# Two norms in front of a SwiGLU: more output blocks in halves, gate products tile by tile, squares summed on TensorE

## The chip, the cores and the metric

The kernel runs on one core of a Trainium2 chip. The metric is the device time of one execution in microseconds (us); a lower time is better. The engines are PE (matrix products; PEld is its weight load), DVE, ACT and POOL (elementwise work), and SP, which here only issues transfers. Every engine works through its own instructions in order; semaphores make one wait for another.

## The reference

One layer of a hybrid encoder over 576 columns (512 of a prompt, 64 of a running stream), model width 1024, feed-forward width 2816:

```python
h = rms_norm(x, g_pre_mix)
p = h @ w_in                       # RWKV-7 rows | gMLP u, v | two gates
o_a = rwkv7(...)                   # recurrence over chunks
o_b = gmlp(...)                    # spatial gating
m = sigmoid(pga) * (o_a @ w_proj_a) + sigmoid(pgb) * (o_b @ w_proj_b)
x = x + rms_norm(m @ w_o, g_post_mix)
f = rms_norm(x, g_pre_ffn)
f = (silu(f @ w_gate) * (f @ w_up)) @ w_down
x = x + rms_norm(f, g_post_ffn)
```

The change lies between `m @ w_o` and the first blocks of `f @ w_gate` and `f @ w_up`.

## The kernel before

All data is transposed: rows of 128 features on the partitions, T = 576 columns beside each other, in two halves of HALF = 288. A product in fp32 precision is made of three cheaper ones: both factors are split into a high part (`h`, `whi`) and the rest (`l`, `wlo`), and high x high, low x high and high x low are added up in PSUM. So a block of 128 output features by one half of the columns takes 8 tiles of 128 input features x 3 = 24 matmuls of 288 columns, and a whole block 48.

**Weights.** `todo` lists the weight blocks in the order of use. `ahead` loads the next one (`raw`) by SP; `split_next()` splits the oldest one that is loaded: ACT writes the high part (L302) and POOL the rest in two pieces of 512 columns (L305), into a ring of three buffers for each (`whi`, `wlo`), or into buffers of its own (`own`, called `s` in the profile). `EARLY` names w_o blocks that are split during the `pb` products (`o_b @ w_proj_b`), and `STEPS` says at which w_o product how many further blocks are split.

**Order.** `behind` writes the second part of the layer down: `pa` and `pb` products, w_o products (`po`), the first gate and up products (`fp`, NF = 2 of 22 blocks), the main loop of them (`fg`), w_down. It is a generator. A planner (`Weave`) runs it beside other generators (`norm1`, `norm2`, `hidden` and more), each of which yields the time or the event at which it is due (`LAT` holds assumed latencies). So the order on PE is the planner's, fixed when the kernel is built. ACT, DVE and POOL take the order that the tile scheduler gives them, except where `keep_in_program_order` pins it.

**w_o and norm1.** `normed_product` computes the first 8 - NLAST blocks whole; then the last NLAST = 5 blocks for the first half of the columns, and then for the second half. `evac1` brings each result from PSUM to `y[j]` (ACT, L1308) and its squares to `zb` (ACT, L1289), which DVE adds up in `gin` (L1290, `acc1`). When a half is done, `norm1(h)` sums the squares over the partitions (three matmuls with one column on a vector of ones, `rs`), takes the power on POOL (`rr`, L368), broadcasts it with three matmuls (`rb`), and then makes, tile by tile, y*rb (DVE, L1321), + x (DVE, L1324), the high part f0h to f7h (ACT, L1325) and the low part f0l to f7l (DVE, L1328). `fcount` counts the tiles that are there.

**First gate products.** For each half, each of the two blocks and gate and up, `half_product("fp", ...)` takes the eight f tiles in order, with one PSUM bank at a time. The four banks of a half come one after the other.

**norm2.** The scale of the second norm (`rs2`) is not applied to f but later, in `swiglu`. For `norm2(h)`, for each y tile, ACT squares it into `zb` and POOL adds it to a second `gin` (`acc2`, L1290 again); then three `rs` matmuls, the power and the broadcast as in norm1. The `hidden` generator starts `swiglu` for the two first blocks once their products and `rs2` are there, and writes their results `d0`, `d1`.

Of the kernel before, what the change touches and what calls it, by code (L numbers as in the profile page):

```python
# [5 lines left out]
F32 = mybir.dt.float32  # L6
F32R = mybir.dt.float32r
ACT = mybir.ActivationFunctionType
ALU = mybir.AluOpType
# [3 lines left out]
P = 128  # L13
D = 1024
TS = 64
TP = 512
T = TS + TP
HALF = T // 2
# [7 lines left out]
KD = D // P  # L26
RMS_EPS = 1e-6
# [206 lines left out]
def layer(tc, I, O):  # L234
# [3 lines left out]
    pe, dve, act, pool, sp = nc.tensor, nc.vector, nc.scalar, nc.gpsimd, nc.sync  # L238
# [7 lines left out]
    nb = {"a": 4}  # L246
# [15 lines left out]
    def ps1(name, hold=0.0):  # L262
        clk.take(hold)
        return psum.tile([P, 512], F32, tag="a", bufs=nb["a"], name=name)
# [7 lines left out]
    def mmul(out, lhsT, rhs, **kw):  # L272
        n = 1
        for d in rhs.shape[1:]:
            n *= d
        rows = lhsT.shape[0]
        if rows != clk.rows:
            clk.now += 0.12
            clk.rows = rows
        if rhs.dtype == F32R:  # L280
            clk.now += 0.011 + n / 2400
        elif rows == P:
            clk.now += max(n, P) / 600
        else:
            clk.now += n / 2000 if rows == 64 else 0.037 if rows == 32 else 0.02
        return pe.matmul(out, lhsT, rhs, **kw)  # L286
# [69 lines left out]
    def rstd_cols(out, m, sq, starts, s=None, more=None):  # L356

        s = ps1("rs") if s is None else s  # L360
        n = len(starts)
        for j, t0 in enumerate(starts):
            mmul(s[:, j:j + 1], sq[:, t0:t0 + P], one, start=True, stop=more is None)
            if more is not None:
                mmul(s[:, j:j + 1], more[:, t0:t0 + P], one, start=False, stop=True)
            clk.now += 0.1
        dve.tensor_scalar(m[:, 0:n], s[:, 0:n], 1.0 / D, RMS_EPS, ALU.mult, ALU.add)
        pool.tensor_tensor(out[:, 0:n], m[:, 0:n], mhalf[:, 0:n], ALU.pow)  # L368
# [19 lines left out]
    def until(*ev):  # L388
        while ev not in clk.events:
            yield True  # L390
# [669 lines left out]
    def slot(i, dt=F32):  # L1060

        return R["gp"].tile([P, D], dt, tag=f"s{i}", bufs=1, name=f"s{i}")
# [49 lines left out]
    def mixed(name, **kw):  # L1112
        return R["mp"].tile([P, T], F32, tag=name, name=name, **{"bufs": 1, **kw})
# [105 lines left out]
            yield LAT["zz"]  # L1219


    NLAST, NF = 5, 2
    EARLY = {3: 6, 5: 7}
    STEPS = {(0, 0): 1, (1, 0): 1, (2, 0): 2, (3, 0): 1, (4, 1): 1, (5, 1): 1, (6, 1): 1, (7, 1): 1}

    def own(i):
        return lambda: (slot(2 * i, F32R), slot(2 * i + 1, F32R))

    todo = [(("w_proj_a", j), I["w_proj_a"][j], None) for j in range(8)]
    for j in range(8):  # L1230
        todo.append((("w_proj_b", j), I["w_proj_b"][j], None))
        if j - 1 in EARLY:
            i = EARLY[j - 1]
            todo.append((("w_o", i), I["w_o"][i], own(i - 6)))
    todo += [(("w_o", j), I["w_o"][j], None) for j in range(6)]
    todo += [((n, j), I[n][j], own(0) if (j, n) == (NF - 1, "w_up") else None) for j in range(NFF) for n in ("w_gate", "w_up")]
    last_w = lambda k0: lambda: [R["op"].tile([P, min(KD, NFF - k0) * P], F32R, name=f"w{k0}{n}") for n in "hl"]
    todo += [(("w_down", j), I["w_down"][j][:, k0 * P:min(k0 + KD, NFF) * P], last_w(k0) if j == 6 else None) for j in range(8) for k0 in range(0, NFF, KD)]
# [15 lines left out]
    def half_product(name, wb, xs, kts, h, step=None, ready=lambda k: True, cut=HALF):  # L1254
        dst = psum.tile([P, 512], F32, tag="h", bufs=6, name=name)[:, 0:(cut, T - cut)[h]]
        for k in range(kts):
            while not ready(k):
                yield True
            if step is not None and k % KD == 0:
                step()  # L1260
            mm({h: dst}, wb, xs[0], xs[1], k, kts, halves=(h,), cut=cut)
            yield
        return dst
# [19 lines left out]
    def square_sum(q, acc, src, first, hs, eng=dve):  # L1283

        if first:
            act.activation(acc[:, hs], src, ACT.Square)
        else:
            q = q()
            act.activation(q[:, hs], src, ACT.Square)  # L1289
            eng.tensor_tensor(acc[:, hs], acc[:, hs], q[:, hs], ALU.add)  # L1290

    def rstd_row(p, acc, starts, tag, more=None):

        m = p.tile([P, 3], F32, tag=tag + "m", bufs=2, name="rm")
        r = p.tile([P, 3], F32, tag=tag + "r", bufs=2, name="rr")
        rstd_cols(r, m, acc, starts, more=more)
        yield LAT["rb"]
        b = ps1("rb")
        for j, t0 in enumerate(starts):
            t0 -= starts[0]  # L1300
            mmul(b[:, t0:t0 + P], r[:, j:j + 1].broadcast_to([P, P]), ident, start=True, stop=True)
        return b[:, 0:starts[-1] + P - starts[0]]

    mix_q = lambda: mixed("zb", bufs=2)
    y, xt = [], []

    def evac1(j, ps, hs):
        act.activation(y[j][:, hs], ps, ACT.Copy, scale=V("g_post_mix", j))  # L1308
        square_sum(mix_q, R["acc1"], ps, j == 0, hs)

    fcount = [0, 0]

    def norm1(h):
        hs = HS[h]
        yield (("po", h), LAT["rs"])
        b = yield from rstd_row(R["fp"], R["acc1"], STARTS[h], "r1")
        keep = tc.keep_in_program_order
        fh, fl = fs
        for j in range(10):
            if j < 8:  # L1320
                keep(dve.tensor_tensor(y[j][:, hs], y[j][:, hs], b, ALU.mult))  # L1321
            if 1 <= j < 9:
                i = j - 1
                keep(dve.tensor_tensor(y[i][:, hs], y[i][:, hs], xt[i][:, hs], ALU.add))  # L1324
                act.activation(fh[i][:, hs], y[i][:, hs], ACT.Copy, scale=V("g_pre_ffn", i))  # L1325
            if j > 1:
                i = j - 2
                keep(dve.scalar_tensor_tensor(fl[i][:, hs], y[i][:, hs], V("g_pre_ffn", i), f(fh[i][:, hs]), ALU.mult, ALU.subtract))  # L1328
                fcount[h] = i + 1
            yield LAT["f0"] if j == 0 else LAT["f"]  # L1330
        clk.signal("y", h)

    def norm2(h):
        hs = HS[h]
        yield (("y", h), 0.0)
        for j in range(8):
            square_sum(mix_q, R["acc2"], y[j][:, hs], j == 0, hs, pool)
            yield LAT["sq"]
        yield LAT["rs"]
        b = yield from rstd_row(R["fp"], R["acc2"], STARTS[h], "r2")  # L1340
        act.activation(R["rs2"][:, hs], b, ACT.Copy)
        clk.signal("rs2", h)


# [50 lines left out]
    def norm3(h):  # L1395
        hs = (slice(0, CUT), slice(CUT, T))[h]
        yield (("pd", h), LAT["rs"])
        y2, x1 = R["yw"][:, :, hs], R["xw"][:, :, hs]
        b = yield from rstd_row(R["op"], R["acc3"], ENDS[h], "r3", R["sq7"])
        keep = tc.keep_in_program_order  # L1400
        for j0, j1, eng in ((0, 2, pool), (2, 4, pool), (4, 6, dve), (6, 8, dve)):
            js = slice(j0, j1)
            keep(dve.tensor_tensor(y2[:, js], y2[:, js], b.unsqueeze(1).broadcast_to([P, j1 - j0, hs.stop - hs.start]), ALU.mult))
            keep(eng.tensor_tensor(y2[:, js], y2[:, js], x1[:, js], ALU.add))
            sp.dma_start(O["yT"][js, :, hs].rearrange("j p t -> p j t"), y2[:, js])


    def behind(ws, split_next):
# [1 line left out]
        clk.signal("behind")  # L1410
        ps_es.close()
        ps_es, psum = mk("ps2", space=PSUM)
        nb["a"] = 2
        ps1("rs")

        def pa_done(j, t, ps):
            o = half_sum(j)
# [28 lines left out]
            dve.tensor_tensor(ma[j], ma[j], t, ALU.add)  # L1446
            keepers(ms, split(R["mp"], ma[j], f"m{j}", scale=0.5))
        y[:] = [half_sum(j) for j in range(8)]
        R["acc1"], R["acc2"] = [mixed("gin", bufs=2) for _ in range(2)]
        R["rs2"] = R["fp"].tile([P, T], F32, name="rs2")  # L1450
        for j in range(8):
            if j < 3:
                xt.append(slot(4 + j))
            elif j < 5:
                xt.append(R["mp"].tile([P, D], F32, tag=("bias", "wsT")[j - 3], bufs=1, name="xt"))
            elif j < 7:
                xt.append(mixed("xt", bufs=2))
            else:
                xt.append(R["fp"].tile([P, T], F32, name="xt"))
            sp.dma_start(xt[j][:, 0:T], I["xT"][:, j, :])  # L1460
# [4 lines left out]
        for j in range(NF):  # L1465
            for x, n in zip(ds, "hl"):
                x.append(R["dp0"].tile([P, T], F32R, name=f"d{j}{n}"))
        for h in range(2):
            for j in range(NF):
                halfway[h, j] = []  # L1470
                for n in ("w_gate", "w_up"):
                    if (h, j, n) == (1, 1, "w_gate"):
                        yield from until("d", 0, 0)
                    if h == 1:
                        yield from until("y", 0)
                    ps = yield from half_product("fp", ws[n, j], fs, KD, h, None, lambda k: fcount[h] > k)
                    halfway[h, j].append(ps)
                    if h == 1:
                        split_next()
                clk.signal("fp", h, j)  # L1480
        for j in range(NF, NFF):
            pgu = []
# [56 lines left out]
```

## Time and profile before

| | us |
|---|---|
| median of 3 runs | 1239.83 (1239.71 to 1240.45) |
| profiled execution | 1237.7 |
| its span | 1235.9 |
| mean granted clock of PE | 0.984 |
| first gate product to first of the main loop | 786.90 to 824.76 |

A row of the timeline gives start, length, engine, line and operation with the tiles that it writes and reads (`fp<-f4l,whi`: into fp from f4l and the weights whi), and in brackets how long the engine was idle before it and what ended that. All matmuls have the line L286, that of a helper. Lengths of matmuls overlap; starts tell their pace. PEclk is the clock granted to PE, 1.00 being full.

### The profile page before, as it was taken

The numbers are of one execution on the slowest core, as the hardware profiler recorded it, in microseconds if no ns is written. First come the engines' busy times: TensorE is split into PE (matmuls) and PEld (weight loads), VectorE is DVE, ScalarE is ACT, GpSimd is POOL, SyncE is SP. The second block draws the span as 40 slices with busy tenths as digits, with TensorE's granted clock in tenths as the row PEclk, the third lists the DMA queues.
The fourth block names the chain that finished last, engine by engine and source line by source line (L and its number), as shares of the span: only waits on it lengthen the run. The fifth ranks groups of instructions, "written<-read, shape, count | busy, mean of one in ns | idle before, by whom it ended". The sixth has DMA issues, their size and how long they took to land.

```text
span 1235.9 us, 29949 instructions
## 1 busy us (share of the span) xinstructions
PE 1187.6 (96%) x12926; PEld 1154.5 (93%) x12926; DVE 547.8 (44%) x1081; ACT 466.1 (38%) x889; POOL 614.1 (50%) x484
## 2 busy tenths in 40 slices
PE   7989999989999989899899999899999999999997
PEld 6989898889899989899899999899999999999996
DVE  5756556665555565632624431654333333300003
ACT  5555544443545434333431233442222222222220
POOL 6665354635354545333445553566565555634442
PEclk9999999998999999999999999899999999999998
DMA  5233222222222222231554542232222222252222
GB/s 184 81 106 90 72 82 85 73 70 67 72 82 85 82 63 72 79 97 63 174 173 129 181 141 86 69 128 85 74 82 86 86 86 85 69 168 83 78 77 77
DMA packets 68276, 118.05 MB, mean 96 GB/s; under 512 B 30832, under 2 KB 36208, under 8 KB 68144
## 3 DMA queue, kind: packets, MB, share of 16 engines
q1 hardware_dynamic: 68000, 116.06, 30.9%
q8 instruction: 101, 1.65, 0.6%
q14 instruction: 31, 0.25, 0.1%
q10 hardware_dynamic: 144, 0.08, 0.0%
HBM read 99.83 MB, written 16.28 MB: 94 GB/s over the span
## 4 chain that ended last, share of the span: by engine, by line
PE 76%; DVE 13%; ACT 3%; issue 3%; POOL 3%; DMA 2%; SPq 0%; DVEq 0%; POOLq 0%; ACTq 0%
PE fg L286 20%; PE pj L286 16%; PE po L286 15%; PE pb L286 4%; PE gv L286 4%; PE pa L286 3%; POOL wlo L305 2%; DVE X L865 2%; DVE Xt L862 2%; PE am L286 2%; PE z L286 1%; PE d L286 1%; DVE TD L965 1%; PE pc L286 1%; DVE y L1324 1%
## 5 line engine op out<-in xcount | busy, mean ns | idle before, releaser
L305 POOL TENSOR_TENSOR wlo<-raw,whi 128x512 fp32r<-128x512 f32 (+1 forms) x288 | 400.5, 1413 | 374.2 <-ACT whi L302 344.3
L302 ACT ACTIVATE whi<-raw 128x1024 fp32r<-128x1024 f32 x144 | 149.7, 1046 | 279.6 <-PE fg L286 174.6
L1290 DVE TENSOR_TENSOR rs<-rs,nsq 128x288 f32<-128x288 f32 (+2 forms) x12 | 9.0, 754 | 105.9 <-ACT nsq L1289 105.9
L1358 DVE TENSOR_TENSOR ft<-ft,fg 128x288 f32<-128x288 f32 x40 | 16.4, 451 | 68.0 <-PE fg L286 66.5
L1352 DVE TENSOR_TENSOR fg<-fg,rs 128x288 f32<-128x288 f32 x40 | 16.5, 453 | 63.2 <-PE fg L286 63.1
L1355 DVE SCALAR_TENSOR_TENSOR ft<-ft,fg 128x576 f32<-128x576 f32 (+1 forms) x24 | 28.7, 1197 | 19.0 <-ACT ft L1354 19.0
L1356 POOL TENSOR_TENSOR ft<-ft,rs 128x576 f32<-128x576 f32 (+1 forms) x24 | 31.8, 1327 | 7.1 <-DVE ft L1355 7.1
L286 PE MATMUL pc<-S,TD 128*128 128x64 f32 x112 | 20.9, 270 | 13.1 <-DVE So L1004 10.8
L286 PEld LDWEIGHTS pc<-S,TD 128*128 128x128 f32 x112 | 18.3, 198 | 15.6 <-DVE So L1004 12.2
L865 DVE TENSOR_TENSOR X<-X,Xt 80x15 f32<-80x15 f32 (+7 forms) x120 | 29.4, 245 | 3.9
L862 DVE TENSOR_TENSOR Xt<-X,M 80x15 f32<-80x15 f32 (+7 forms) x120 | 29.3, 245 | 3.6
L1035 POOL TENSOR_TENSOR gm<-gm,mhalf 128x10 f32<-128x10 f32 x8 | 16.2, 2022 | 27.3 <-DVE gm L1034 27.2
L1004 DVE TENSOR_TENSOR S<-pc,C 128x64 f32<-128x64 f32 x48 | 10.5, 219 | 42.8 <-PE pc L286 42.8
L286 PE MATMUL pj<-h5h,whi 128*128 128x288 f32 x88 | 28.4, 323 | 0.0
L765 POOL TENSOR_TENSOR BK<-BK,EL 128x576 f32<-128x576 f32 x16 | 19.8, 1238 | 16.9 <-PE am L286 16.9
L286 PE MATMUL pj<-h0h,whi 128*128 128x288 f32 x88 | 28.2, 320 | 0.0
L286 PE MATMUL pj<-h6h,whi 128*128 128x288 f32 x88 | 28.1, 320 | 0.0
L286 PE MATMUL pj<-h3h,whi 128*128 128x288 f32 x88 | 27.9, 317 | 0.0
L286 PE MATMUL pj<-h7h,whi 128*128 128x288 f32 x88 | 27.7, 315 | 0.0
L286 PE MATMUL pj<-h1h,whi 128*128 128x288 f32 x88 | 27.6, 314 | 0.0
L286 PE MATMUL pj<-h2h,whi 128*128 128x288 f32 x88 | 27.6, 314 | 0.0
L286 PE MATMUL pj<-h4h,whi 128*128 128x288 f32 x88 | 27.6, 313 | 0.0
(1200 smaller groups left out, 4281.4 us busy)
## 6 DMA issues: line engine op xcount, KB each, us to landing
raw<-in_w_in SPq DMA_DIRECT2D x50, 512.0 KB, 3.7
raw<-in_w_gate SPq DMA_DIRECT2D x22, 512.0 KB, 3.7
raw<-in_w_up SPq DMA_DIRECT2D x22, 512.0 KB, 3.6
raw<-in_w_down SPq DMA_DIRECT2D x16, 512.0 KB, 3.5
raw<-in_w_gv SPq DMA_DIRECT2D x8, 512.0 KB, 3.6
raw<-in_w_proj_a SPq DMA_DIRECT2D x8, 512.0 KB, 3.8
raw<-in_w_proj_b SPq DMA_DIRECT2D x8, 512.0 KB, 3.7
raw<-in_w_o SPq DMA_DIRECT2D x8, 512.0 KB, 3.7
```

Source lines behind the costliest of these rows:

```text
L286: return pe.matmul(out, lhsT, rhs, **kw)
L302: keep(act.activation(hi[:, :cols], raw[:, :cols], ACT.Copy))
L305: keep(pool.tensor_tensor(lo[:, c0:c1], raw[:, c0:c1], f(hi[:, c0:c1]), ALU.subtract))
L765: pool.tensor_tensor(by_chunk(BK[:, x, :]), by_chunk(BK[:, x, :]), EL[:, :, 64:65].broadcast_to([P, NCH, 64]), ALU.mult)
L862: ins = dve.tensor_tensor(t3, X[:, 0:r, s:s + 1].broadcast_to([NU, r, w]), M[:, s:s + 1, s + 1:SB].broadcast_to([NU, r, w]), ALU.mult)
L865: dve.tensor_tensor(X[:, 0:r, s + 1:SB], X[:, 0:r, s + 1:SB], t3, ALU.add)
L965: dve.tensor_tensor(TD[rows, cs, rows], ps[rows, :, 1, :], by_place[rows, cs, 0, :], ALU.add)
L1035: pool.tensor_tensor(m, m, mhalf, ALU.pow)
L1352: keep(dve.tensor_tensor(g[:, HS[h]], pg, rs2[:, HS[h]], ALU.mult))
L1355: keep(dve.scalar_tensor_tensor(t[:, ts], t[:, ts], 1.0, g[:, ts], ALU.add, ALU.mult))
L1356: pool.tensor_tensor(t[:, ts], t[:, ts], rs2[:, ts], ALU.mult)
L1358: dve.tensor_tensor(t[:, HS[h]], t[:, HS[h]], pu, ALU.mult)
```

## The change

It has four parts. NLAST goes from 5 to 6, so that w_o blocks 2 to 7 are computed in halves; a further w_o block is split early, `STEPS` shifts, and three of the x tiles use other buffers. In norm1 the squares of block 7 are not added by DVE but kept (`rmask`'s buffer) and given to PE: the `rs` sum of a half is six one-column matmuls in place of three. In norm2 ACT squares each y tile as before, POOL adds nothing, and PE sums each tile's squares with three one-column matmuls that accumulate in a PSUM bank. And the first gate and up products go tile by tile: each f tile of the first half is used for both blocks, gate and up, in four banks, before the next tile; in the second half block 0 goes first, then block 1.

```diff
-    NLAST, NF = 5, 2
-    EARLY = {3: 6, 5: 7}
-    STEPS = {(0, 0): 1, (1, 0): 1, (2, 0): 2, (3, 0): 1, (4, 1): 1, (5, 1): 1, (6, 1): 1, (7, 1): 1}
+    NLAST, NF = 6, 2
+    EARLY = {1: 5, 3: 6, 5: 7}
+    STEPS = {(0, 0): 1, (1, 0): 2, (2, 0): 1, (3, 1): 1, (4, 1): 1, (5, 1): 1, (6, 1): 1}
...
+    norm_bank = lambda i: psum.tile([P, 512], F32, tag=f"n{i}", bufs=1, name="rs")
...
     def evac1(j, ps, hs):
+        if j == 7:
+            act.activation(last_sq[:, hs], ps, ACT.Square)
         act.activation(y[j][:, hs], ps, ACT.Copy, scale=V("g_post_mix", j))
-        square_sum(mix_q, R["acc1"], ps, j == 0, hs)
+        if j < 7:
+            square_sum(mix_q, R["acc1"], ps, j == 0, hs)
...
-        b = yield from rstd_row(R["fp"], R["acc1"], STARTS[h], "r1")
+        b = yield from rstd_row(R["fp"], R["acc1"], STARTS[h], "r1", last_sq)
...
     def norm2(h):
...
         yield (("y", h), 0.0)
-        for j in range(8):
-            square_sum(mix_q, R["acc2"], y[j][:, hs], j == 0, hs, pool)
+        if h == 1:
+            yield (("rs2", 0), 0.0)
+        else:
+            R["s2"] = norm_bank(1)
+        s2 = R["s2"]
+        sums = s2[:, HALF:HALF + len(starts)]
+        qs = []
+        for j in range(9):
+            if j < 8:
+                q = mixed("zb", bufs=2)
+                act.activation(q[:, hs], y[j][:, hs], ACT.Square)
+                qs.append(q)
             yield LAT["sq"]
-        yield LAT["rs"]
-        b = yield from rstd_row(R["fp"], R["acc2"], STARTS[h], "r2")
-        act.activation(R["rs2"][:, hs], b, ACT.Copy)
+            if j > 0:
+                for i, t0 in enumerate(starts):
+                    mmul(sums[:, i:i + 1], qs[j - 1][:, t0:t0 + P], one, start=(i, j) == (0, 1), stop=j == 8, skip_group_check=True)
+        m, r = [R["fp"].tile([P, 3], F32, tag="r2" + n, bufs=2, name="r2" + n) for n in "mr"]
+        dve.tensor_scalar(m, sums, 1.0 / D, RMS_EPS, ALU.mult, ALU.add)
+        pool.tensor_tensor(r, m, mhalf[:, 0:3], ALU.pow)
+        yield LAT["rb"]
...
-                xt.append(slot(4 + j))
+                xt.append(wp.tile([P, T], F32, tag="st", bufs=3, name="xt"))
...
-        for h in range(2):
-            for j in range(NF):
-                halfway[h, j] = []
-                for n in ("w_gate", "w_up"):
-                    if (h, j, n) == (1, 1, "w_gate"):
-                        yield from until("d", 0, 0)
...
-                    ps = yield from half_product("fp", ws[n, j], fs, KD, h, None, lambda k: fcount[h] > k)
-                    halfway[h, j].append(ps)
-                    if h == 1:
-                        split_next()
+        for h, js in ((0, (0, 1)), (1, (0,)), (1, (1,))):
+            if (h, js) == (1, (1,)):
+                yield from until("d", 0, 0)
+            for j in js:
+                halfway[h, j] = [psum.tile([P, 512], F32, tag="h", bufs=6, name="fp")[:, 0:HALF] for _ in range(2)]
+            for k in range(KD):
+                while fcount[h] <= k:
+                    yield True
+                for j in js:
+                    for n, ps in zip(("w_gate", "w_up"), halfway[h, j]):
+                        mm({h: ps}, ws[n, j], fs[0], fs[1], k, KD, halves=(h,))
+                        yield
+            for j in js:
+                if h == 1:
+                    split_next(2)
                 clk.signal("fp", h, j)
```

The first place to look at is the start of the gate products on PE. Numbers behind the names tell buffers apart; fp_10921 and its like are PSUM banks, `cst` holds the vector of ones. Before:

```order
L286 MATMUL fp_10921<-f0h_10335,whi_10739 128x288
L286 MATMUL fp_10921<-f0l_10336,whi_10739 128x288
L286 MATMUL fp_10921<-f0h_10335,wlo_10740 128x288
L286 MATMUL fp_10921<-f1h_10337,whi_10739 128x288
L286 MATMUL fp_10921<-f1l_10338,whi_10739 128x288
L286 MATMUL fp_10921<-f1h_10337,wlo_10740 128x288
```

And now:

```order
L286 MATMUL rs_10903<-cst_64,zb_10904 128x1 x3
L286 MATMUL fp_10931<-f0h_10342,whi_10711 128x288
L286 MATMUL fp_10931<-f0l_10343,whi_10711 128x288
L286 MATMUL fp_10931<-f0h_10342,wlo_10712 128x288
L286 MATMUL fp_10932<-f0h_10342,whi_10752 128x288
L286 MATMUL fp_10932<-f0l_10343,whi_10752 128x288
L286 MATMUL fp_10932<-f0h_10342,wlo_10753 128x288
L286 MATMUL rs_10903<-cst_64,zb_10912 128x1 x3
L286 MATMUL fp_10933<-f0h_10342,whi_10799 128x288
L286 MATMUL fp_10933<-f0l_10343,whi_10799 128x288
```

One bank took f0, f1 and so on; now f0 goes into bank after bank, and a group of norm2 (`zb` of y0, then of y1) stands ahead of every six products.

The second place is ACT at the end of norm1's first half. The tiles y[0], y[1], ... are y_10308, y_10309, ... before and y_10316, y_10317, ... now. Before:

```order
L1325 ACTIVATE f5h<-y_10313,vec 128x288
L1308 ACTIVATE y_10315<-po,vec 128x288
L1289 ACTIVATE zb<-po 128x288
L1289 ACTIVATE zb<-y_10309 128x288
L1325 ACTIVATE f6h<-y_10314,vec 128x288
L1325 ACTIVATE f7h<-y_10315,vec 128x288
L1289 ACTIVATE zb<-y_10310 128x288
```

And now:

```order
L1332 ACTIVATE f5h<-y_10321,vec 128x288
L1314 ACTIVATE y_10322<-po,vec 128x288
L1289 ACTIVATE zb<-po 128x288
L1354 ACTIVATE zb<-y_10316 128x288
L1332 ACTIVATE f6h<-y_10322,vec 128x288
L1332 ACTIVATE f7h<-y_10323,vec 128x288
L1354 ACTIVATE zb<-y_10317 128x288
L1313 ACTIVATE rmask<-po 128x288
L1314 ACTIVATE y_10323<-po,vec 128x288
L1354 ACTIVATE zb<-y_10318 128x288
```

The squares of y0 stand where those of y1 stood, and those of y1 come behind f6h and f7h; PE, not POOL, waits for them now.

The third place is POOL around the power that ends norm2. Before (`rr` for both norms):

```order
L1290 TENSOR_TENSOR gin<-gin,zb 128x288 x7
L368 TENSOR_TENSOR rr<-rm,mhalf 128x3
L1290 TENSOR_TENSOR gin<-gin,zb 128x288 x5
L1356 TENSOR_TENSOR ft<-ft,rs_10318 128x288
L305 TENSOR_TENSOR wlo<-raw,whi 128x512 x4
L1356 TENSOR_TENSOR ft<-ft,rs_10318 128x288
L305 TENSOR_TENSOR wlo<-raw,whi 128x512 x2
L368 TENSOR_TENSOR rr<-rm,mhalf 128x3
```

And now (`r2r` for norm2):

```order
L368 TENSOR_TENSOR rr<-rm,mhalf 128x3
L1362 TENSOR_TENSOR r2r<-r2m,mhalf 128x3
L1382 TENSOR_TENSOR ft<-ft,rs_10325 128x288 x2
L305 TENSOR_TENSOR wlo<-raw,whi 128x512 x4
L1362 TENSOR_TENSOR r2r<-r2m,mhalf 128x3
L1382 TENSOR_TENSOR ft<-ft,rs_10325 128x288
```

The adds are gone, and the second power stands behind four pieces of weights of the main loop.

More of the change, by code (lines that the diff above doesn't have):

```diff
@@ L1233, in layer @@
             i = EARLY[j - 1]
-            todo.append((("w_o", i), I["w_o"][i], own(i - 6)))
-    todo += [(("w_o", j), I["w_o"][j], None) for j in range(6)]
+            todo.append((("w_o", i), I["w_o"][i], own(i - 5)))
+    todo += [(("w_o", j), I["w_o"][j], None) for j in range(5)]
     todo += [((n, j), I[n][j], own(0) if (j, n) == (NF - 1, "w_up") else None) for j in range(NFF) for n in ("w_gate", "w_up")]
@@ L1290, in square_sum, with rstd_row @@
             eng.tensor_tensor(acc[:, hs], acc[:, hs], q[:, hs], ALU.add)
-    def rstd_row(p, acc, starts, tag, more=None):
+    norm_bank = lambda i: psum.tile([P, 512], F32, tag=f"n{i}", bufs=1, name="rs")
+    def rstd_row(p, acc, starts, tag, more=None, bank=0):
         m = p.tile([P, 3], F32, tag=tag + "m", bufs=2, name="rm")
         r = p.tile([P, 3], F32, tag=tag + "r", bufs=2, name="rr")
-        rstd_cols(r, m, acc, starts, more=more)
+        rstd_cols(r, m, acc, starts, norm_bank(bank), more)
         yield LAT["rb"]
-        b = ps1("rb")
+        b = norm_bank(bank)
         for j, t0 in enumerate(starts):
@@ L1305, in layer @@
     y, xt = [], []
+    last_sq = rmask.rearrange("p c t -> p (c t)")
     def evac1(j, ps, hs):
+        if j == 7:
+            act.activation(last_sq[:, hs], ps, ACT.Square)
         act.activation(y[j][:, hs], ps, ACT.Copy, scale=V("g_post_mix", j))
-        square_sum(mix_q, R["acc1"], ps, j == 0, hs)
+        if j < 7:
+            square_sum(mix_q, R["acc1"], ps, j == 0, hs)
     fcount = [0, 0]
@@ L1333, in norm2 @@
     def norm2(h):
-        hs = HS[h]
+        hs, starts = HS[h], STARTS[h]
         yield (("y", h), 0.0)
-        for j in range(8):
-            square_sum(mix_q, R["acc2"], y[j][:, hs], j == 0, hs, pool)
-            yield LAT["sq"]
-        yield LAT["rs"]
-        b = yield from rstd_row(R["fp"], R["acc2"], STARTS[h], "r2")
-        act.activation(R["rs2"][:, hs], b, ACT.Copy)
+        if h == 1:
[10 more added lines that the diff above has]
+                qs.append(q)
+            yield LAT["sq"]
+            if j > 0:
[5 more added lines that the diff above has]
+        yield LAT["rb"]
+        for j, t0 in enumerate(starts):
+            t0 -= starts[0]
+            mmul(s2[:, t0:t0 + P], r[:, j:j + 1].broadcast_to([P, P]), ident, start=True, stop=True)
+        act.activation(R["rs2"][:, hs], s2[:, 0:HALF], ACT.Copy)
         clk.signal("rs2", h)
@@ L1398, in norm3 @@
         y2, x1 = R["yw"][:, :, hs], R["xw"][:, :, hs]
-        b = yield from rstd_row(R["op"], R["acc3"], ENDS[h], "r3", R["sq7"])
+        b = yield from rstd_row(R["op"], R["acc3"], ENDS[h], "r3", R["sq7"], h)
         keep = tc.keep_in_program_order
@@ L1412, in behind @@
         ps_es, psum = mk("ps2", space=PSUM)
-        nb["a"] = 2
-        ps1("rs")
+        norm_bank(0)
+        norm_bank(1)
         def pa_done(j, t, ps):
@@ L1448, in behind @@
         y[:] = [half_sum(j) for j in range(8)]
-        R["acc1"], R["acc2"] = [mixed("gin", bufs=2) for _ in range(2)]
+        R["acc1"] = mixed("gin", bufs=2)
         R["rs2"] = R["fp"].tile([P, T], F32, name="rs2")
@@ L1467, in behind @@
                 x.append(R["dp0"].tile([P, T], F32R, name=f"d{j}{n}"))
-        for h in range(2):
-            for j in range(NF):
-                halfway[h, j] = []
-                for n in ("w_gate", "w_up"):
-                    if (h, j, n) == (1, 1, "w_gate"):
-                        yield from until("d", 0, 0)
-                    if h == 1:
-                        yield from until("y", 0)
-                    ps = yield from half_product("fp", ws[n, j], fs, KD, h, None, lambda k: fcount[h] > k)
-                    halfway[h, j].append(ps)
-                    if h == 1:
-                        split_next()
+        for h, js in ((0, (0, 1)), (1, (0,)), (1, (1,))):
[13 more added lines that the diff above has]
+                    split_next(2)
                 clk.signal("fp", h, j)
```

## The prediction

> **What bounds the kernel now.** I read the page first, for the engine that could be the bound.
>
> ```profile
> PE 1187.6 (96%) x12926; PEld 1154.5 (93%) x12926; DVE 547.8 (44%) x1081; ACT 466.1 (38%) x889; POOL 614.1 (50%) x484
> ```
>
> PE, the matmuls, is busy for 96% of the span. So the question is whether the 4% that is left lies where the change works, and what the change gives PE to do. The table by stretches answers the first half. Its columns are busy time and instruction count of each engine, then the granted clock.
>
> ```profile
> core 0: us, PE busy (x) PEld busy (x) DVE busy (x) ACT busy (x) POOL busy (x), PEclk, DMA share, GB/s
> 760.00:786.00 26.00, 26.00 (x200) 26.00 (x199) 10.58 (x19) 10.29 (x21) 9.11 (x8) 1.00 0.21 62
> 790.00:800.00 10.00, 7.02 (x30) 6.58 (x31) 5.05 (x8) 4.18 (x11) 7.71 (x9) 0.69 0.18 52
> 800.00:810.00 10.00, 10.00 (x76) 10.00 (x76) 8.07 (x19) 4.40 (x11) 4.71 (x7) 0.97 0.39 148
> 810.00:825.00 15.00, 14.69 (x109) 13.99 (x108) 7.89 (x15) 7.27 (x14) 10.24 (x11) 1.00 0.39 129
> 825.00:860.00 35.00, 34.79 (x260) 34.32 (x259) 14.91 (x25) 10.67 (x15) 19.81 (x16) 1.00 0.26 77
> ```
>
> Ahead of the first gate products (the w_o products, 760 to 786) PE is full, and behind them (from 825) nearly so. Between 790 and 800 it works 7.02 of 10 us, at 0.69 of its clock. What it waits for there is in the list of waits of PE, 736 to 860:
>
> ```profile
> PE fp L286 <- DVE f4l L1328: 2.1, 1, 2.1
> PE fp L286 <- DVE f5l L1328: 1.8, 1, 1.8
> PE rs L286 <- DVE gin L1290: 0.3, 1, 0.3
> PE rb L286 <- POOL rr L368: 0.2, 1, 0.2
> PE fp L286 <- DVE f7l L1328: 0.2, 1, 0.2
> ```
>
> The first gate block needs the normed tiles f0 to f7 faster than DVE makes them. The timeline gives the length of the phase, from its first product (fp) to the first of the main loop (fg), and the broadcast of norm2's second half (rb), which falls just behind:
>
> ```profile
> 786.90 0.30 PE L286 MATMUL fp<-f0h,whi 128*128 128x288 f32 x1
> 824.76 0.42 PE L286 MATMUL fg<-f0h,whi 128*128 128x288 f32 x2
> 828.32 0.93 PE L286 MATMUL rb<-cst,rr 128*128 128x128 f32 x6 [0.21 <-POOL rr L368]
> 829.01 0.51 PE L286 MATMUL fg<-f4h,whi 128*128 128x288 f32 x2
> ```
>
> That is 37.86 us to the first fg; a broadcast costs 829.01 - 828.32 = 0.69. What the phase would take without a stall needs two prices:
>
> ```profile
> 806.40 0.29 PE L286 MATMUL fp<-f1h,s 128*128 128x288 f32 x1
> 806.53 0.72 PE L286 MATMUL rs<-cst,gin 128*128 128x1 f32 x6
> 807.12 0.38 PE L286 MATMUL fp<-f2h,s 128*128 128x288 f32 x1
> 807.33 0.29 PE L286 MATMUL fp<-f2l,s 128*128 128x288 f32 x1
> ...
> 1209.38 0.28 PE L286 MATMUL rs<-cst,rs 128*128 128x1 f32 x2
> 1210.64 0.36 PE L286 MATMUL po<-d7h,w0h 128*128 128x256 f32 x1
> 1210.85 0.28 PE L286 MATMUL po<-d7l,w0h 128*128 128x256 f32 x1
> ```
>
> A product of 288 columns follows the last after 0.132 us (0.13 from 806.40 to 806.53; records overlap, so starts count, not lengths). Three one-column matmuls, a group that adds up squares (rs), push the next products back by 807.33 - 806.53 - 0.13 = 0.67, say 0.66. The group of six near the end costs 1210.85 - 1209.38 - 0.12 = 1.35, twice that. A phase of 2 halves x 2 blocks x gate and up x 8 tiles x 3 = 192 products (25.3), three rs groups (2.0) and two broadcasts (1.4) makes 28.7. So 37.86 - 28.7 = 9.2 us are stalls. The quoted waits are 4.4 of them (2.1 + 1.8 + 0.3 + 0.2). The largest other part is the clock:
>
> ```profile
> 793.80:797.20 3.40, 3.11 (x14) 3.05 (x14) 1.25 (x4) 1.54 (x4) 2.17 (x3) 0.51 0.29 117
> 797.20:800.60 3.40, 3.40 (x16) 3.40 (x15) 0.00 (x0) 1.33 (x3) 3.09 (x5) 0.50 0.00 0
> 800.60:804.00 3.40, 3.40 (x27) 3.40 (x27) 2.07 (x6) 0.84 (x3) 0.41 (x1) 0.99 0.03 9
> ```
>
> After the two waits the granted clock is half for 6.8 us: 3.4 us lost. The other 1.4 us or so are scattered slow starts.
>
> **The change, part by part.** The sum is against the profiled execution, 1237.7 us (span 1235.9), 2.1 under the median of 1239.83; I add the difference to the median.
>
> 1. *norm2's squares on PE.* Fourteen POOL adds and two rs groups go; sixteen rs groups come, so fourteen more: 14 x 0.66 = +9.2 on PE, which has nothing to hide behind. What POOL saves is this row:
>
> ```profile
> L1290 POOL TENSOR_TENSOR gin<-gin,zb 128x288 f32<-128x288 f32 x14 | 11.7, 837 | 8.3 <-ACT zb L1289 7.9
> ```
>
> Nobody waits for it but the 0.2 us of rr above, so 11.7 us less on POOL buy 0.2.
>
> 2. *Block 7's squares unadded in norm1.* Two groups grow from three to six: 2 x (1.35 - 0.66) = +1.4. The DVE add that it saves lies beside PE's work in both halves, except the 0.3 us wait for gin.
>
> 3. *Block 2 in halves.* PE's work is the same, but the first halves of all blocks are done 24 x 0.132 = 3.2 us earlier, less 0.7 for the larger group: the DVE and ACT chain of norm1 shifts by -2.5 us, while the first fp comes 0.7 later (787.6).
>
> 4. *Tile by tile over four banks.* In the first half each f tile carries 12 products (1.6 us) instead of 3 (0.4). With the rs groups among them PE takes about as long for a tile as DVE does. f4 to f7 are then long there when PE comes. This, with 3, removes the waits of the first list: at most all 9.2 + 0.2 = -9.4.
>
> 5. *Early weights.* Block 5 of w_o is split during the pb products, and three x tiles load into other buffers, sooner on SP's queue. One more split on POOL's queue is two pieces of about 1.4 us (four take 5.48 in a row below). The DMA share of 0.21 at 760 to 786 leaves room; whoever comes behind the split on POOL has slack by my reading of the orders. I take 0; from below 0 too (a w_o weight comes sooner, but PE already has no gap there), from above 2.8, both pieces in the open.
>
> The floor of the sum is thus 9.2 + 1.4 - 9.4 = +1.2: even if every stall goes, PE has gained more work than it had waits.
>
> 6. *New waits.* These rows carry them:
>
> ```profile
> 790.23 0.44 ACT L1289 ACTIVATE zb<-y 128x288 f32<-128x288 f32 x1
> 793.70 0.54 ACT L1325 ACTIVATE f7h<-y,vec 128x288 fp32r<-128x288 f32 x1 [0.80 <-DVE y L1324]
> 794.14 0.76 ACT L1289 ACTIVATE zb<-y 128x288 f32<-128x288 f32 x2
> ...
> 790.81 1.52 DVE L1324 TENSOR_TENSOR y<-y,xt 128x288 f32<-128x288 f32 x1
> 793.22 0.44 DVE L1324 TENSOR_TENSOR y<-y,xt 128x288 f32<-128x288 f32 x1
> ...
> 816.37 5.48 POOL L305 TENSOR_TENSOR wlo<-raw,whi 128x512 fp32r<-128x512 f32 x4
> ```
>
> The first rs group of norm2 stands ahead of the first fp. Its squares take the place that 790.23 has on ACT; 2.5 earlier and 0.44 long, they are ready at 788.2, and PE is there at 787.6: 0.6. The second square, of y1, stands on ACT behind f6h and f7h, which wait for DVE's last adds (790.81, 793.22). From 794.14: 791.6 plus 0.4 is 792.0. PE, after 0.66 for a group and six products (0.79), is there at 789.6: 2.4, or 1.8 if ACT runs back to back from f7h; I take 2.0. Queued behind that group are all products of the first half, with f1 to f5 already there. In the second half four POOL pieces for the next blocks' weights (5.48) stand ahead of the power that ends norm2 (r2r). They start when the first of the two blocks is done and end about 1.4 us after PE reaches the broadcast; between 0 (started sooner) and 2.0 I take 1.4. New waits together +4.0, bounds 0 and 5.0. DVE too now waits for PE's sum in the first half (about 1.5 us); f0 of the second half is not due before all 96 products of the first, which covers it; without cover it costs 1.5.
>
> Without the clock: 9.2 + 1.4 - 9.4 + 4.0 = **+5.2**.
>
> 7. *The clock.* Does it halve again? It did so at other places:
>
> ```profile
> 302.06 1.17 PE L286 MATMUL n<-cst,q 128*128 128x2 f32 x10
> 303.57 0.85 PE L286 MATMUL m<-IT,AB 16*32 16x16 f32 x80 [0.34 <-DVE IT L874]
> 304.35 0.40 PE L286 MATMUL pj<-h5h,whi 128*128 128x288 f32 x1
> ...
> 461.81 0.43 PE L286 MATMUL pc<-S,TD 128*128 128x64 f32 x2 [2.28 <-DVE So L1004]
> ...
> 305.70:309.10 3.40, 3.40 (x92) 3.08 (x92) 2.27 (x4) 1.14 (x3) 1.71 (x2) 0.51 0.45 134
> ...
> 53.35 0.40 PE L286 MATMUL pk<-u0h,whi 128*128 128x288 f32 x1 [1.63 <-ACT st L576]
> ```
>
> After 2.3 us (302.06 to 304.35) of tiny matmuls with 0.34 of waiting the clock was half for 3.4 us; after 2.28 of waiting it fell too; after 1.63 it did not. So few-column work counts about as idle. In the new order the stretch from the wait for y1's squares to the end of its group is 2.0 + 0.66 = 2.7 us without a wide product, with a similar one of 1.3 just before it and 2.0 (a group of six and one of three) 0.8 behind. I expect one or two half-clock stretches, 1.7 us lost in each: +1.7 to +3.4, and take the middle, 2.6.
>
> The Trainium skill, in "TensorE: Matmul & The Clock Gate", section "What's actually happening", has the clock halved after at least one idle window of about 3.4 us, and its section "Why this matters for your kernels" asks for no gap over about 3 us. By that no wait here would halve it, and the sum would stay at +5.2. The trace disagrees at 461.81, where 2.28 us were enough.
>
> Sum: 5.2 + 2.6 = +7.8: 1245.5 for an execution like the profiled one, **1247.6** against the median.
>
> **The rivals.**
> - *The clock holds* (+5.2, 1245): the waits come, but each is under the 2.28 that is known to do it. For it: the y1 wait may be 1.8. Against: the tiny matmuls around it.
> - *The mix keeps it halved* (+10 to +16, 1250 to 1256): rs groups and six products alternate through f0 to f3; at half clock six products take 1.6 and a group about 1.3, so wide work is some 54% of the time. From 793.80 to 797.20 a stretch with nearly as little did not bring the clock back. Three stretches lost (5.1) give +10; the whole of some 11 us of mixed work doubled gives +16.
> - *Break even* (+1.2, 1241): squares come in time, no new wait; the change then pays its PE work with the old stalls. That is the case in which it does what it says.
> - *Faster*: a one-column matmul hides in the shadow of the wide product before it, and takes one slot of 0.132 like any other: a group is then 0.40, and 16 group equivalents (14 and the two growths) save 16 x 0.26 = 4.2. With the floor of 1.2 that is -3.0: 1236.8. It decides from 0.43 a group on, and only if all waits go too. Against it stands the 0.66 measured among just such products.
> - *The earlier split stalls pb* (+2.8 on top, 1250).
>
> **How the numbers follow.** Clock halved once or twice: 0.38. Clock holds: 0.22. Stays halved: 0.18. Break even: 0.11. Faster: 0.05. Split stalls pb: 0.06. A measurement of this kernel tells about 0.2%, 2.5 us, from no change: break even is inside (same 0.11), faster 0.05, the rest slower, 0.84. The likeliest case alone spans 1246 to 1249. Eight in ten: from 1240.5, which leaves out the faster case and a little of break even, to 1254, which leaves out the upper third of the halved mix.
>
> **What would show it.** Right: no wait for f4l or f5l; waits of PE at rs for ACT's squares near 788 and 790, together about 2.6; 0.66 a group; from first fp (or rs) to the broadcast of the second half about 44 us at full clock where it was 38.7; PEclk under 1 between 790 and 800. Wrong: PE groups of less than 0.45; y1's squares ahead of PE; a PEclk of 1.00 throughout (then +5); or new gaps ahead of 786, which I count at nothing.

## The result, and the profile after

The changed kernel takes 1255.63 us in the median (1254.14 to 1257.41, 4 runs) against 1239.77 before (1237.27 to 1240.45, 4 runs): +15.9 us, a ratio of 1.0132 with a 95% interval from 1.0112 to 1.0152. It is slower, as forecast, but by twice the forecast +7.8 and above the range, which ended at 1254. The two profiled executions differ by 19.7, more than the medians; the clock also falls at places ahead of the change, and more often in this execution (half for 34 us before 790, against 24). The time is that of the rival "the mix keeps it halved" (1250 to 1256). The profiled execution after took 1257.41 us (span 1255.6), 1.8 above its median.

The list of PE's waits after, 736 to 880 us, against the five rows of before:

```profile
PE rs L286 <- ACT zb L1354: 2.3, 2, 1.6
PE rs L286 <- POOL r2r L1362: 1.3, 1, 1.3
```

No product waits for a tile of norm1 any more; the new waits are at the sums of norm2. The timeline of PE shows them one by one, and the first product of the main loop:

```profile
790.69 0.83 PE L286 MATMUL rs<-cst,zb 128*128 128x1 f32 x6 [0.63 <-ACT zb L1354]
794.07 1.44 PE L286 MATMUL rs<-cst,zb 128*128 128x1 f32 x6 [1.65 <-ACT zb L1354]
...
843.11 0.93 PE L286 MATMUL rs<-cst,r2r 128*128 128x128 f32 x6 [1.28 <-POOL r2r L1362]
...
846.25 0.43 PE L286 MATMUL fg<-f0h,whi 128*128 128x288 f32 x2
```

The waits are 0.63, 1.65 and 1.28 us; 0.6, 2.0 and 1.4 had been foreseen. PE was free for the sum at 790.06, so the phase up to the main loop, its last broadcast included, takes 56.2 us, against 38.8 before (37.86, and 0.90 for the wait and the broadcast at 828). The table by stretches has the reason in its column PEclk, the seventh:

```profile
790.29:793.70 3.41, 1.73 (x12) 1.50 (x12) 3.41 (x6) 1.44 (x5) 1.71 (x2) 1.00 0.15 34
...
787.00:793.70 6.70, 4.79 (x35) 4.33 (x34) 6.70 (x13) 4.01 (x9) 2.72 (x2) 1.00 0.35 95
793.70:821.00 27.30, 26.93 (x119) 26.93 (x120) 9.57 (x26) 7.38 (x17) 1.70 (x2) 0.50 0.21 81
821.00:846.00 25.00, 23.72 (x188) 23.49 (x188) 5.59 (x13) 8.37 (x17) 7.43 (x7) 1.00 0.20 66
...
814.20:817.60 3.40, 3.40 (x17) 3.40 (x17) 1.90 (x6) 0.98 (x2) 0.85 (x1) 0.50 0.05 18
817.60:821.00 3.40, 3.40 (x16) 3.40 (x16) 3.28 (x9) 1.07 (x2) 0.00 (x0) 0.50 0.65 249
```

PE is busy for 26.93 of 27.3 us, so no list of waits shows the loss: the clock is half for 27.3 us (6.8 before), which is 13.65 us lost where it was 3.4. The halved stretches of these traces, but for one that runs into the end of the kernel, last 3.4, 6.8, 10.2 or 27.3 us: one, two, three or eight steps of 3.41. The first row is the step ahead of the fall, in which PE waits for 3.41 - 1.73 = 1.68 us; the last two are the seventh and the eighth step of half clock. The same mix of six products and one group of sums runs at both clocks, in the first half of the columns and in the second:

```profile
806.23 1.28 PE L286 MATMUL rs<-cst,zb 128*128 128x1 f32 x6
808.95 1.27 PE L286 MATMUL rs<-cst,zb 128*128 128x1 f32 x6
811.67 1.27 PE L286 MATMUL rs<-cst,zb 128*128 128x1 f32 x6
814.39 1.27 PE L286 MATMUL rs<-cst,zb 128*128 128x1 f32 x6
...
829.05 0.72 PE L286 MATMUL rs<-cst,zb 128*128 128x1 f32 x6
830.52 0.72 PE L286 MATMUL rs<-cst,zb 128*128 128x1 f32 x6
831.98 0.72 PE L286 MATMUL rs<-cst,zb 128*128 128x1 f32 x6
```

One period is 2.72 us up to the group at 814.39, the last of the first half, and 1.46 us from 827.59 on. With 0.79 for six products, 0.67 is left for a group, the price that the sum took. From 815.53, where that last group is done, there are products alone. So six of the eight steps hold the mix, the seventh holds one group and two thirds products (2.3 of 3.4 us), and the clock is back at the end of the eighth, the first with products alone (817.60:821.00).

### The profile page after: what moved, and what is told of

It reads as the page before. It is cut to its first block, busy times and chain, and to the rows that moved or that the text cites. A ratio compares the mean times of both kernels' runs of the same rounds, so it can differ in the third digit from the quotient of the medians.

```text
span 1255.6 us, 30127 instructions
## 1 busy us (share of the span) xinstructions
PE 1208.3 (96%) x13022; PEld 1176.6 (94%) x13022; DVE 544.9 (43%) x1079; ACT 467.5 (37%) x889; POOL 602.9 (48%) x470
## 4 chain that ended last, share of the span: by engine, by line
PE 77%; DVE 12%; issue 4%; POOL 3%; ACT 3%; DMA 1%; SPq 0%; DVEq 0%; POOLq 0%; ACTq 0%
PE fg L286 20%; PE pj L286 16%; PE po L286 14%; PE pb L286 4%; PE gv L286 4%; PE pa L286 3%; POOL wlo L305 2%; PE fp L286 2%; PE rs L286 2%; DVE X L865 2%; DVE Xt L862 2%; PE am L286 2%; PE z L286 1%; PE d L286 1%; DVE TD L965 1%
```

## The experiments

Theory A: matmuls with one column count for PE's clock as if PE stood idle. Together with the waits at the start they halve it, and at half clock the mix has too little wide work (products of 288 columns) to bring it back. Its main rivals: the waits alone do it, whatever the width; or the mix itself, without a wait.

Each time stands against runs of the kernel before in the same session (medians 1237.5 to 1237.9). PEclk falls also at places outside the change, and not equally often in every profile; single executions of the kernel before lay between 1230.8 and 1240.8. What a run shows of its own place is therefore read from the phase in its profile, and the times from medians.

**Wider sums in norm2.** The matmul's second factor, one column of ones, is repeated 64 times, and DVE reads one of the 64 equal sums (not shown below); nothing else changes.

```diff
-        sums = s2[:, HALF:HALF + len(starts)]
+        sums = s2[:, HALF:HALF + 64 * len(starts)]
-                    mmul(sums[:, i:i + 1], qs[j - 1][:, t0:t0 + P], one, ...)
+                    mmul(sums[:, 64 * i:64 * i + 64], qs[j - 1][:, t0:t0 + P], one.broadcast_to([P, 64]), ...)
```

> The changed kernel, but each sum of norm2 on PE is taken 64 times over (64 equal columns in place of one; DVE reads one of them). The weight load of 128 columns stays, and a broadcast of three 128-column matmuls took 0.69 us against 0.66 for a group of three one-column ones, so the groups should cost about the same. Theory A, few-column matmuls count as idle for PE's clock: with wide ones the clock comes back, the half-clock stretch behind 786 us shrinks from 27.3 us to 0 to 6.8, and the time is 1243 to 1248. Theory B, what holds the clock down is not the width (the gaps between weight loads, fp32 itself, or the waits alone): half clock stays near 27 us and the time at 1254 to 1257.

1248.03 us, ratio 1.0091 (1.0061 to 1.0121). Its table by stretches:

```profile
792.70:802.90 10.20, 10.20 (x48) 10.20 (x47) 0.16 (x1) 1.40 (x4) 0.86 (x1) 0.51 0.01 4
802.90:836.00 33.10, 31.79 (x252) 31.55 (x252) 14.34 (x36) 13.42 (x27) 8.29 (x8) 1.00 0.29 104
```

The halved stretch is 10.2 us in place of 27.3, with PE's instructions the same in number and order, and waits of 2.0 and 1.3 us at the same places. Width matters, against theory B of the expectation; but 10.2 is above the 6.8 that A allowed.

**Norm2's first half later.** One number in the planner moves the groups behind the first tiles:

```diff
-        yield (("y", h), 0.0)
+        yield (("y", h), 0.0 if h else 6.0)
```

> The changed kernel, with norm2's first half due 6 us later in the planner, so that its groups stand from the fourth tile on and no longer ahead of the first products. The waits for the squares of y0 and y1 (0.6 and 1.65 us) go; a wait of up to 2 us at the six-matmul group of norm1's second half may come instead. Theory A (low-width work and waits together drop the clock; a mix of six products and a group keeps the state that it finds, as the second half shows at full clock): 1242 to 1246, half clock behind 786 us at most 6.8 us. Rival (the mix of the first half drops the clock by itself): over 1250, half clock over 15 us.

1243.86 us, ratio 1.0064 (1.0035 to 1.0093). Its table by stretches:

```profile
788.80:792.20 3.40, 2.15 (x17) 2.09 (x18) 1.75 (x5) 1.69 (x5) 0.24 (x1) 1.00 0.53 154
792.20:795.60 3.40, 3.40 (x17) 3.40 (x16) 0.00 (x0) 0.00 (x0) 0.62 (x1) 0.50 0.02 5
795.60:830.00 34.40, 33.15 (x268) 32.91 (x267) 13.82 (x35) 14.97 (x31) 8.28 (x8) 1.00 0.29 100
```

And rows of its timeline of PE, the last two from norm2's first half:

```profile
789.67 0.35 PE L286 MATMUL rs<-cst,gin 128*128 128x1 f32 x2 [0.96 <-DVE gin L1290]
790.41 0.38 PE L286 MATMUL rs<-cst,rmask 128*128 128x1 f32 x2 [0.38 <-ACT rmask L1313]
...
798.35 0.72 PE L286 MATMUL rs<-cst,zb 128*128 128x1 f32 x6
799.82 0.72 PE L286 MATMUL rs<-cst,zb 128*128 128x1 f32 x6
```

The clock falls once, at norm1's second group (waits of 0.96 and 0.38 us in front of and within six one-column matmuls). The stretch that follows holds wide products alone, and it is back after 3.4 us; the mix that comes then keeps full clock, all of it, in the first half of the columns too. So the mix does not drop the clock by itself; it keeps what it finds. One of nine executions took 1256.96 us at a mean clock of 0.974, where the others had 0.982 to 0.986 and at most 1244.8. That would fit a mix that met half clock and stayed there; the execution has no profile, so this is not shown.

**Norm1's second sum later as well.** In addition to the last edit:

```diff
-        yield (("po", h), LAT["rs"])
+        yield (("po", h), LAT["rs"] + 4.0 * h)
```

> As the run with norm2's first half later, and norm1's second group 4 us later as well, so that PE should meet no wait between 780 and 800 us while all 16 groups stay in the mix of six products and a group. Theory A: no half clock behind 780 us at all, and what is left is the added PE work: 14 x 0.66 + 1.4 - 9.4 = +1.2, with 1.3 for the wait at the power of the second half +2.5: 1239 to 1241 against 1237.5 of before. Rival (the mix drops the clock by itself): half clock returns, above 1245.

1239.86 us, ratio 1.0015 (1.0004 to 1.0025). In its profile PE waits for nothing between 770 and 860:

```profile
786.00:800.00 14.00, 14.00 (x111) 14.00 (x110) 7.98 (x16) 6.04 (x14) 3.69 (x4) 1.00 0.26 76
800.00:830.00 30.00, 30.00 (x244) 30.00 (x243) 14.19 (x34) 14.38 (x29) 9.20 (x9) 1.00 0.34 115
```

With all 16 groups in place, no wait and full clock, it is 2.1 us above before: the floor of the sum (+1.2) within the interval (+0.5 to +3.1). The 10.6 us of work that PE gained are not quite won back even then.

**All sums of both norms widened,** to 64 columns and then to 128, in the order of the changed kernel. Norm2's sums change as in the first experiment; the helper below serves norm1, and the last norm near 1209 as well.

```diff
+        w = 128 if more is not None else 1        # 64 in the first of the two runs
...
-            mmul(s[:, j:j + 1], sq[:, t0:t0 + P], one, ...)
+            o = one if w == 1 else one.broadcast_to([P, w])
+            mmul(s[:, w * j:w * j + w], sq[:, t0:t0 + P], o, ...)
```

> As the run with 64 equal columns in norm2's sums, and norm1's and norm3's sums of six matmuls widened in the same way. In that run the first half-clock stretch still held the six one-column matmuls of norm1 (2.6 us at half clock). Theory A (few columns count as idle): with these wide too, half clock behind 780 us is 3.4 to 6.8 us in place of 10.2, and the time 1.7 to 3.4 us less: 1244 to 1246. Rival (width is not it): as the changed kernel, above 1253.

> As the run with all sums of both norms widened, with 128 equal columns in place of 64, the width of the broadcasts (0.69 us for three, 1.28 at half clock, against 0.66 and 1.27 of one-column groups), so hardly longer. Theory A, now with a threshold: at half clock six products took 1.45 us and a group of 64 columns 1.38 of which about half the time streams columns, so some 75% of the stretch was wide work, and three stretches passed; with 128 columns nearly all of it is wide, so that the clock should be back after one stretch or two: half clock 3.4 to 6.8 us, 1244 to 1248. If it stays at 10.2, columns beyond 64 do not count and something else (the start of the weights' stream, fp32 passes) holds it; if at 27, the 64-column results were chance.

At 64 columns the time is 1249.6 us, ratio 1.0095 (1.0073 to 1.0117), and half clock again 10.2 us: that expectation missed, norm1's width on top of norm2's buys nothing. From its table by stretches, the step ahead of the fall and the halved stretch:

```profile
790.20:793.60 3.40, 1.75 (x14) 1.52 (x14) 3.18 (x6) 1.95 (x5) 0.84 (x1) 0.98 0.44 113
793.60:803.90 10.30, 10.30 (x48) 10.30 (x48) 0.16 (x1) 1.80 (x5) 0.85 (x1) 0.51 0.04 15
```

At 128 columns the time is 1243.1 us, ratio 1.0048 (1.0029 to 1.0066), and the clock does not fall between 787 and 832. Its waits of PE:

```profile
PE rs L286 <- ACT zb L1356: 2.2, 2, 1.7
PE rs L286 <- POOL r2r L1364: 1.4, 1, 1.4
```

The stretch of the whole phase, with PEclk 1.00, and a stretch that holds its longest wait:

```profile
787.00:832.00 45.00, 41.39 (x329) 40.70 (x328) 19.85 (x46) 18.91 (x41) 12.20 (x12) 1.00 0.26 93
789.64:793.05 3.41, 1.75 (x14) 1.53 (x13) 2.77 (x6) 2.36 (x6) 0.43 (x1) 1.00 0.45 154
```

And two groups in its timeline:

```profile
795.06 0.83 PE L286 MATMUL rs<-cst,zb 128*128 128x128 f32 x6
796.53 0.83 PE L286 MATMUL rs<-cst,zb 128*128 128x128 f32 x6
```

This is the run that decides. It has the waits of the changed kernel (2.2 and 1.4 against 2.3 and 1.3), the same groups at the same places, a period of 1.47 us against 1.46, and only the columns differ. Without them the clock is half for 27.3 us, with them for none. One rival has still to be ruled out: halved stretches start on a grid of such steps, so the same waits could fall into one step in one execution and be shared by two in another. In the trace of the changed kernel the halved stretches at 602.56 and 793.70 start 191.14 us apart, 56 steps of 3.413. In this run's trace one starts at 601.9, and 55 such steps later come 789.64 to 793.05, the step in the row above. PE is busy in it for 1.75 us, as in the step ahead of the fall with 64 columns (1.75) and with one (1.73). So the steps were nearly alike, and the clock fell behind two of them and not behind the third. The five executions, 1242.2 to 1246.6 us, also lie clear of the changed kernel's four (1254.1 and more), though only one of them has a profile. These waits alone do not halve the clock (the longer ones of before, 2.1 and 1.8 us, had); one-column work added to them does. The time also lies at 1237.9 + 5.2, the sum without the clock.

**Thinner groups.** Norm2's groups 18 to 21 products apart:

```diff
-            yield LAT["sq"]
+            yield LAT["sq"] if j < 2 else 2.6
```

> The changed kernel with norm2's groups on PE thinned out: 18 to 21 products between two of them in place of 6, so wide work is about 80% of the time in place of 53%. Waits stay at the start (0.6 at the squares of y0, about 2 in all at norm1's second group with 2 us of one-column work behind). Theory A (the clock halves at the waits, and returns if enough of a half-clock stretch is wide work; 53% is not enough): the clock drops and is back after one or two stretches, half clock 3.4 to 6.8 us, 1241 to 1246. Rival (any one-column group in a half-clock stretch keeps it there): 15 us or more, above 1249.

1257.47 us, ratio 1.0158 (1.0145 to 1.0171): neither theory's number, for a reason of its own.

```profile
PE fp L286 <- DVE ft L1384: 3.8, 1, 3.8
PE rs L286 <- POOL r2r L1362: 2.2, 2, 1.5
```

The clock did not fall at the start at all, where the waits were shorter (1.0 and 0.2 us), so the question was not put there. But norm2 ends late (its broadcast for the first half waits for the power until 816.28), the first SwiGLU block needs its scale, and its PSUM banks come free late: PE waits 3.8 us for them at 822.6, and there the clock falls, for 10.2 us, and for 10.2 again behind 844. The last two steps of the first of these say something of the return:

```profile
824.00:827.40 3.40, 3.40 (x16) 3.40 (x16) 1.23 (x3) 1.22 (x3) 0.79 (x1) 0.50 0.06 25
827.40:830.80 3.40, 3.40 (x16) 3.40 (x15) 0.14 (x1) 0.00 (x0) 0.00 (x0) 0.50 0.00 0
```

The first holds one group (at half clock 1.13 us, from 824.97 to the next product at 826.10) and is else products, two thirds of it, and the clock stayed at half, as in the seventh step of the changed kernel. The second holds products alone, and the clock came back. The run also shows the price of a late norm2, on which the prediction had nothing.

**Norm2 on POOL as before,** the other parts kept; and **the tile order alone,** on the kernel before.

> The changed kernel, with norm2 as before (POOL adds the squares, one group of three on PE for a half); six blocks in halves, norm1's six matmuls and the products tile by tile stay. Added on PE 1.4 us, stalls of up to 9.4 removed, a wait of about 2 us at norm1's second group, perhaps one half-clock stretch (1.7): 1233 to 1237, so faster than before. If the tile order or the bank use cost time by themselves, it is above 1239.8.

> The kernel before with only the order tile by tile over four banks. The waits for f4l and f5l go (each tile now feeds 12 products), but norm1's second group stands after 18 products, about 789.3 us, and its last sum was there at 794.0 before: a wait of up to 4.7 us, with one or two half-clock stretches behind it. 1235 to 1240. If it is near 1231, that wait did not come.

1235.7 us, ratio 0.998 (0.9955 to 1.0004), and 1236.91, ratio 0.9997 (0.9972 to 1.0021): neither can be told from before. Both lie in their expected ranges; that the first is faster than before, as was expected too, is not shown. It shows that the loss comes with norm2's sums on PE (1255.6 with them). Why the stalls that were taken away (up to 9.4) bring so little is in the lists of PE's waits, 770 to 860. With norm2 on POOL:

```profile
PE rs L286 <- DVE gin L1290: 1.6, 1, 1.6
PE fp L286 <- DVE ft L1365: 1.0, 1, 1.0
PE rs L286 <- ACT rmask L1313: 0.7, 1, 0.7
```

With the tile order alone:

```profile
PE rs L286 <- DVE gin L1290: 2.4, 1, 2.4
PE fg L286 <- DVE ft L1358: 1.1, 1, 1.1
PE fp L286 <- ACT s L302: 1.0, 1, 1.0
PE fp L286 <- POOL s L305: 0.8, 1, 0.8
```

The waits for f4l and f5l are gone, and PE comes too early for the next inputs: norm1's second sum, and in the tile order alone the fourth weight block, which is now needed with the first tile. Behind it the clock is half for 3.4 and 6.8 us.

**Moving norm1's second sum later,** with norm2 on POOL; the second of these also has three matmuls a sum again.

```diff
-        yield (("po", h), LAT["rs"])
+        yield (("po", h), LAT["rs"] + 3.0 * h)
...
-        yield LAT["rs"]
+        yield LAT["rs"] + 5.0 * (1 - h)
```

> Norm2 on POOL as before, the rest of the change kept, and the sum of norm1's second half moved 24 products later, behind its last squares, norm2's first sum later too. The waits of 1.6 and 0.7 us and the half-clock stretch of the run with norm2 on POOL go (4.0 us in all); DVE's f tiles of the second half bound the next products instead and give back 1 or 2. 1232 to 1235 against 1237.5 of before: faster. If DVE bounds it wholly: 1236.

> As the run before it in this list, with norm1's sums back at three matmuls a half (DVE adds the squares of block 7 again): 1.4 us less on PE, 0.45 us more on DVE in each half. PE's part: -1.4; if DVE's f tiles bound the second half, +0.4. 1231 to 1235.

1242.8 us (ratio 1.0038, 1.0026 to 1.005) and 1241.56 (1.0033, 1.0021 to 1.0045): slower, not faster. The wait came back later, at the start of the main loop. From the list of waits of the first of the two (the second has 4.4 us in the same row):

```profile
PE fg L286 <- DVE ft L1365: 4.3, 1, 4.3
```

**Squares of norm2's first half on DVE,** which idles there, and norm1's second sum 12 products later; then the same with the sums a little later yet.

```diff
-            square_sum(mix_q, R["acc2"], y[j][:, hs], j == 0, hs, pool)
+            square_sum(mix_q, R["acc2"], y[j][:, hs], j == 0, hs, pool if h else dve)
...
-        yield (("po", h), LAT["rs"])
+        yield (("po", h), LAT["rs"] + 1.6 * h)      # then 2.2 here, and LAT["rs"] + 1.0 * (1 - h) for norm2
```

> The run with norm2 on POOL, with the squares of norm2's first half added by DVE (idle there for some 5 us) and norm1's second sum 12 products later. POOL's seven adds stood ahead of norm1's second power, which came 2.4 us after its input; that goes. The waits of 1.6 and 0.7 us and the half-clock stretch of 3.4 (1.7 lost) should go too. The chain of DVE's f tiles and of the first SwiGLU block comes some 2.4 us earlier and sets the gain: 1233 to 1235 against 1237.6 of before. If that chain does not move: 1236.

> As the run before it in this list, with the sums 0.6 and 1 us later yet, by which POOL does both of the first SwiGLU products before the four weight pieces, and norm2's second power before the next four. If POOL's order bounds the start of the main loop, 1 to 3 us less than the run before it: 1231 to 1234. If DVE does: no difference.

The first takes 1235.15 us, ratio 0.9984 (0.9968 to 0.9999), the only version here that is measurably faster than both kernels, if only just: by 2.8 us. Its clock is full from 788 to 826. The second takes 1241.17, ratio 1.0021 (1.0003 to 1.0039), against its expectation. POOL's timeline of it has part of the cause:

```profile
820.03 5.02 POOL L305 TENSOR_TENSOR wlo<-raw,whi 128x512 fp32r<-128x512 f32 x4 [1.99 <-ACT whi L302]
825.00 0.86 POOL L368 TENSOR_TENSOR rr<-rm,mhalf 128x3 f32<-128x3 f32 x1
827.27 5.32 POOL L305 TENSOR_TENSOR wlo<-raw,whi 128x512 fp32r<-128x512 f32 x4 [1.40 <-ACT whi L302]
832.55 0.79 POOL L1363 TENSOR_TENSOR ft<-ft,rs 128x288 f32<-128x288 f32 x1
```

And DVE's and PE's:

```profile
830.18 1.29 DVE L1362 SCALAR_TENSOR_TENSOR ft<-ft,fg 128x288 f32<-128x288 f32 x1 [1.31 <-ACT ft L1361]
833.37 0.45 DVE L1365 TENSOR_TENSOR ft<-ft,fp 128x288 f32<-128x288 f32 x1 [1.90 <-POOL ft L1363]
...
833.88 0.61 PE L286 MATMUL fg<-f0h,whi 128*128 128x288 f32 x1 [4.56 <-DVE ft L1365]
```

The planner's number that freed the first two SwiGLU products of POOL's queue put four weight pieces in front of the third one (832.55), and PE waits 4.56 us for what hangs on it. The pieces are not all of it: DVE's input to that product was ready at 830.18 + 1.29 = 831.47, so they hold it for 1.1 us. DVE's row at 833.37 came at 829.57 in the first version, 3.8 us sooner; the rest of the delay arises ahead of POOL, in the sums, which are 1.2 later (823.31 against 822.08), and on ACT and DVE. Those shares were not tested apart.

## Why the prediction was right and wrong

- *Parts 1 and 2, +9.2 and +1.4.* Right: 0.67 a group in the changed kernel, and +2.1 us left in the run without a wait, where the floor of the sum was +1.2.
- *Parts 3 and 4, the old waits go.* Right: none of the five old rows is in the list after.
- *Part 5, early weights at nothing.* Nothing speaks against it: with norm2 on POOL the rest of the change costs nothing. It was not run alone.
- *Part 6, new waits of 4.0.* Right: measured 3.6, at the three places that were named.
- *+5.2 without the clock.* Right: the run with 128 columns, at full clock, is +5.2. That it agrees to the tenth is luck; the interval goes from +3.6 to +8.2.
- *Part 7, the clock, +1.7 to +3.4.* Here it failed. That the clock would fall was right, and that few-column work counts as idle. The size was taken from places where mostly wide work followed at once, as at 305.70, so that one or two stretches were the end of it. Here the mix followed, and eight stretches passed (27.3 us, 13.65 lost), seven of them with groups in them. 5.2 + 13.65 gives +18.9, where the phase grew by 17.4 (56.2 - 38.8) and norm1's first sum by 0.7 in front of it; the medians, over other executions, differ by 15.9. The rival that priced this had the row (793.80 to 797.20, which did not bring the clock back at about half wide work), and got 0.18; it should have been the likeliest. It knew what the kernel does next (groups and six products through f0 to f3), and the main case did not: it counted one or two stretches without asking what would end them. Even that rival had at most 11 us lost, as it left out norm1's second sum, the broadcast and the last stretch of products, which run at half clock too.
- *"The clock holds", +5.2.* Wrong for the changed kernel, though by the rule of the Trainium skill ("TensorE: Matmul & The Clock Gate", section "What's actually happening": half clock after at least one idle window of about 3.4 us) no wait here, of 1.65 us at most, would have halved it. The trace disagrees for one-column work beside the waits, and agrees where the sums are 128 wide.

Still open: how much wide work a stretch must hold to bring the clock back. Pure products did so after one stretch, the mix with 64 columns after three, the mix with one column not in six, and two stretches that were two thirds products, one in the changed kernel and one with thinner groups, did not; no run varied this share alone.

## What to carry to other kernels

Before moving a reduction to PE, count not only the microseconds but the columns: one-column matmuls keep the engine "busy" in every list and can leave its clock at half, and with 128 equal columns they took as long and did not. When a profile shows half clock behind a wait, look at what PE does next: wide work alone ended it after one stretch, and a mix held it for six. And a wait that is taken away at one place (f4l, f5l) brings PE sooner to the next input, so the gain is known only once the next two or three due times have been read too.

## What the runs showed of the hardware that was not expected

- The same mix ran at full clock for some 11 us (827 to 839) and at half clock for some 21 (794 to 815): it kept each state that it met.
- Three steps of 3.4 us with the same busy time of PE (1.73, 1.75 and 1.75 us) differed on PE mainly in the columns of their groups: behind 1 and 64 columns the clock fell, behind 128 it did not.
- A group of three fp32 matmuls costs the same 0.67 us with 1 and with 128 columns (periods of 1.46 and 1.47 us with six products).
